# Layer 1's shift and scale columns: eight PE row sums and VectorE steps replaced by one VectorE dot product per column

## The chip, the cores and the metric

The program runs on one core of one Trainium2 chip. TensorE is called PE here, VectorE DVE, ScalarE ACT, GpSimd POOL, and SyncE, whose queue issues nearly all loads, SP. The metric is the device time of one execution in microseconds (us); less is better.

## What is computed

Two decoder layers on 256 tokens of width 1024, both with the same frame: a modulation from the vector `c`, an RMS norm, a mixer, a gated residual. The change is in the modulation of the first layer (`i = 0`) and in the input projection of its mixer:

```python
for i in range(DEPTH):                                  # DEPTH = 2, D = 1024, SEQ = 256
    shift, scale, gate = jnp.split(c @ ada_w[i] + ada_b[i], 3, axis=-1)   # c: (1, 1024), ada_w[i]: (1024, 3072)
    h = rmsnorm(x, norm_g[i]) * (1.0 + scale[:, None, :]) + shift[:, None, :]
    ...
        y = nsa_mixer(h, a_w_in[li], ...)               # layer 0: q, kv, gate_logits, z = split(h @ w_in)
    ...
        y = mlstm_mixer(h, b_w_in[li], ...)             # layer 1
    x = x + gate[:, None, :] * y
return rmsnorm(x, final_g)
```

`shift` and `scale` are two vectors of 1024 numbers, each a dot product of `c` with a column of `ada_w[0]`. The kernel needs them transposed: for each of eight blocks `kk` of 128 channels, a column `[128, 2]` with the channel on the partition.

## The kernel before

The order of every engine's instructions in layer 1 is the order in which the code is written (`manual_schedule`); in layer 2 a scheduler sets it. Weights come in float32 through one stream, issued by SP in the order of `self.queue`. A load lands in one of ten buffers named `raw`, or in a guest place that is free at the time (`homes`: tiles `Q`, `KH`, `KL`), and waits for that buffer's last reader. For the matmuls each weight is split into a high part `wh` (ACT, line 162, `make_hi`) and a low part `wl` (DVE, line 167, `make_lo`), and so is the activation: `hh[:, kk]` high, `hl[:, kk]` low. A product is then three matmuls: `wh*hh`, `wl*hh`, `wh*hl`.

`setup` starts the loads of `x`, of `pca` (which holds `c` as eight columns, the norm weights and the biases of the modulation) and fills PE with idle matmuls (`warm`) of 512 columns each.

`first_phase` makes the norm and the projection `proj(kk)` for the eight blocks `kk` of 128 input channels. A block has 42 matmuls of 256 tokens at line 452: 24 for the 1024 outputs of the `q` weight (eight with `wh`, eight with `wl`, eight with `hl`), and 18 for the 768 outputs of the `s` weight. All of them sum into seven PSUM banks over the eight blocks. Before a block can start, its `hh[:, kk]` must be there, and for that its two columns `cols`.

The columns are made in three ways:

- Block 0: the weights of shift and scale (`opening`, input channel on the partition) are multiplied by `crep` (each number of `c` repeated 32 times) on PE, sixteen narrow matmuls in `ada_rows` (line 224) that leave four partial rows in four groups of partitions; a DVE copy; and a matmul with `sel` (line 471) that sums the groups and turns the row into a column.
- Block 1: the same inside block 0's matmuls (after matmul 21 `ada_rows`, after matmul 26 the turn at line 534, then `hh[:, 1]` on DVE).
- Blocks 2 to 7: `rows` (lines 405, 407). The weights (`pairs`, two loads of 512 KB per block) hold, per input channel on the partition, 128 shifts and 128 scales for each of four groups of input channels. Two ACT steps and six DVE steps multiply the eight groups by their number of `c` and sum them into two tiles `adaA` `[128, 256]`; line 512 adds the two. `columns` sums over the partitions with two PE matmuls with `ones1` (line 413), and two ACT steps (lines 415, 416) add the bias and scale. In block `kk` this is done for block `kk + 1`, the PE part after matmul 28 (32 in block 1). `modulate` then makes `hh[:, kk + 1]` on ACT (line 420).

After the eighth block the keys and values follow (`kv_block`, lines 593 to 595 and 1636 to 1638, weights `keys`), then the attention and layer 2.

Of the kernel before, what the change touches and what calls it, by code (L numbers as in the profile page):

```python
# [11 lines left out]
AF = mybir.ActivationFunctionType  # L12
OP = mybir.AluOpType
# [10 lines left out]
class Kernel:  # L24
# [223 lines left out]
    def setup(self):  # L248
# [13 lines left out]
        self.warm(10)  # L262
# [58 lines left out]
    def layer1(self):  # L321
        nc, t, pc, p1 = self.nc, self.t, self.pc, self.p1
        ident = self.ident
        self.stream_init()
        place = [[] for _ in range(KC)]

        def ada(kk):
            if kk > 1:
                self.pairs_stream(kk)
            else:  # L330
                self.cols_stream(kk)
            if kk:
# [36 lines left out]
        self.small_loads()  # L369

        with self.tc.manual_schedule(engines={mybir.EngineType.PE, mybir.EngineType.Activation, mybir.EngineType.DVE, mybir.EngineType.Pool, mybir.EngineType.SP}):
            self.first_phase(place)
            self.nsa(self.acc)
            self.boundary()

    def first_phase(self, place):
# [6 lines left out]
        self.warm(8)  # L383
# [15 lines left out]
        def rows(A, n):  # L399

            raw = self.take_raw(1)[0]
            for j in range(4):
                w, c, acc = raw[:, j].rearrange("p b m -> p (b m)"), pca[:, 4 * n + j : 4 * n + j + 1], A[:, j % 2]
                if not n and j < 2:
                    nc.scalar.activation(acc, w, AF.Copy, scale=c)
                else:
                    nc.vector.scalar_tensor_tensor(acc, w, c, acc, op0=OP.mult, op1=OP.add)

        def columns(kk, A):

            bank = self.bank(7)
            for b in (1, 0):
                nc.tensor.matmul(bank[:, b : b + 1], A[:, 0, b * P : b * P + P], self.ones1, start=True, stop=True, skip_group_check=True)
# [28 lines left out]
        def proj(kk):  # L442
# [3 lines left out]
            for i, m in ((0, 0), (0, 1), (0, 2), (1, 0), (1, 2), (1, 1)) if 0 < kk < KC - 1 else ((0, 0), (0, 1), (0, 2), (1, 0), (1, 1), (1, 2)):  # L446
# [35 lines left out]
        nc.vector.tensor_copy(*copies[1])  # L482
# [5 lines left out]
        A1 = self.T(pc, [P, 512], tag="adaA", bufs=2)  # L488
        for kk in range(KC):

            if not kk:
                self.make_lo(*wide)
# [4 lines left out]
            ahead = 0 < kk < KC - 1  # L497
            if ahead:
                A = self.T(pc, [P, 512], tag="adaA", bufs=2).rearrange("p (h m) -> p h m", h=2)
            if kk > 1 and ahead:  # L500
                rows(A, 0)
# [4 lines left out]
            if kk == 1:  # L506
                rows(A, 0)
            if kk == 1:
                wide = self.make_hi(place[kk][1])
            if ahead:  # L510
                rows(A, 1)
                nc.vector.tensor_tensor(A[:, 0], A[:, 0], A[:, 1], op=OP.add)
            if kk == 1:
                self.make_lo(*wide)
            elif kk:
                self.make(place[kk][1])
# [7 lines left out]
            for n, _ in enumerate(proj(kk)):  # L524
                if (kk, n) == (7, 8):
                    parameters()
                if not kk and n == 21:
                    bank, raws = self.bank(7), self.take_raw(2)
                    self.ada_rows(bank, raws, SEQ)
                    nc.vector.tensor_copy(A1[:, 0:SEQ], bank[:, 0:SEQ])  # L530
                if not kk and n == 26:
                    cols, bank = self.T(pc, [P, 2], tag="cols", bufs=4), self.bank(7)
                    for b in (1, 0):
                        nc.tensor.matmul(bank[:, b : b + 1], A1[:, b * P : b * P + P], self.sel[:, 0:1], start=True, stop=True, skip_group_check=True)
                    for b in (1, 0):
                        column(bank, cols, b, 1)
                    nc.vector.tensor_scalar(self.hh[:, 1], xT[:, 1], cols[:, 1:2], cols[:, 0:1], op0=OP.mult, op1=OP.add)
                    self.make_lo(*parts)
                elif 0 < kk < KC - 1 and n == (32 if kk == 1 else 28):
                    cols = columns(kk + 1, A)  # L540
# [477 lines left out]
    def cols_stream(self, kk):  # L1018

        for b in range(2):  # L1020
            self.add(None, [P, KC, P], self.t["opening"][2 * kk + b])
# [5 lines left out]

    def pairs_stream(self, kk):

        for h in range(2):  # L1030
            self.add(None, [P, 4, 2, P], self.t["pairs"][2 * (kk - 2) + h])
# [646 lines left out]
def layout(inputs):  # L1678
# [17 lines left out]
    out["opening"] = flat([modulation[0][:, :, b, P * kk : P * kk + P] for kk in range(2) for b in range(2)])  # L1696
    out["pairs"] = flat([modulation[0][:, 4 * h : 4 * h + 4, :, P * kk : P * kk + P] for kk in range(2, KC) for h in range(2)])
# [22 lines left out]
```

## Time and profile before

| | |
|---|---|
| median of 3 runs | 443.38 us (442.69 to 443.74) |
| the profiled execution | 442.93 us, its span from the first to the last instruction 441.1 us |
| PE busy | 431.9 us, 98% of the span |
| DVE busy | 338.5 us, 77% |
| ACT busy | 279.0 us, 63% |
| blocks 0 to 7 of the projection | 12.92 to 58.87 us of the span |
| keys and values | 58.87 to about 78 us |

The profile shows one execution, in us from the start of its span. A group's row has the line, engine, operation, tiles and shapes, the count, the busy time, the mean ns of one, and the idle time of the engine just ahead with what ended it. A row of the timeline has start, duration, engine, line and count; the square bracket has the idle time ahead and its releaser. A table of windows has, for each stretch, its length and each engine's busy time with the number of instructions. PE durations overlap, since matmuls are pipelined; a price on PE is therefore taken from start to start. A float32 matmul shows as two rows (its count in the profile is twice that in the program), a matmul of the split parts as one.

### The profile page before, as it was taken

The numbers are of one execution on the slowest core, as the hardware profiler recorded it, in microseconds if no ns is written. First come the engines' busy times: TensorE is split into PE (matmuls) and PEld (weight loads), VectorE is DVE, ScalarE is ACT, GpSimd is POOL, SyncE is SP. The second block draws the span as 40 slices with busy tenths as digits, with TensorE's granted clock in tenths as the row PEclk, the third lists the DMA queues.
The fourth block names the chain that finished last, engine by engine and source line by source line (L and its number), as shares of the span: only waits on it lengthen the run. The fifth ranks groups of instructions, "written<-read, shape, count | busy, mean of one in ns | idle before, by whom it ended". The sixth has DMA issues, their size and how long they took to land.

```text
span 441.1 us, 8017 instructions
## 1 busy us (share of the span) xinstructions
PE 431.9 (98%) x2919; PEld 369.5 (84%) x2919; DVE 338.5 (77%) x771; ACT 279.0 (63%) x563; POOL 37.6 (9%) x92
## 2 busy tenths in 40 slices
PE   8999999999999999999999999999999999999993
PEld 3999999689578877788899799988888888888883
DVE  4899899788787677788995398789886977558553
ACT  4677693876887786459657775554665565455521
POOL 4000030224232020021000000000000000000000
PEclk9999999999999999999999999999999999999997
DMA  8999877782387777826864536638646766530002
GB/s 281 417 415 419 299 239 245 276 315 66 124 318 275 285 270 253 289 103 207 292 211 152 164 123 219 208 128 269 227 143 189 258 243 230 183 137 1 0 1 96
DMA packets 27031, 94.56 MB, mean 214 GB/s; under 512 B 3216, under 2 KB 3232, under 8 KB 26992
## 3 DMA queue, kind: packets, MB, share of 16 engines
q1 hardware_dynamic: 26352, 92.30, 59.3%
q0 software_dynamic: 352, 0.97, 0.8%
q10 hardware_dynamic: 288, 0.79, 0.7%
q8 instruction: 23, 0.38, 0.3%
q14 instruction: 16, 0.13, 0.1%
HBM read 93.00 MB, written 1.05 MB: 213 GB/s over the span
## 4 chain that ended last, share of the span: by engine, by line
PE 89%; DVE 4%; DMA 3%; ACT 1%; issue 1%; SPq 0%; DVEq 0%
PE bank L595 10%; PE bank L593 10%; PE bank L594 10%; PE bank L1638 6%; PE bank L1637 6%; PE bank L1636 6%; PE bank L914 5%; PE bank L1547 5%; PE bank L1077 5%; PE bank L1191 4%; PE bank L452 3%; PE bank L224 3%; PE bank L866 3%; PE bank L849 3%; DMA raw<-in_keys 2%; PE bank L1427 2%
## 5 line engine op out<-in xcount | busy, mean ns | idle before, releaser
L167 DVE TENSOR_TENSOR wl<-raw,wh 128x1024 fp32r<-128x1024 f32 (+4 forms) x127 | 137.3, 1099 | 40.2 <-ACT wh L162 39.3
L162 ACT ACTIVATE wh<-raw 128x1024 fp32r<-128x1024 f32 (+4 forms) x127 | 118.6, 956 | 64.1 <-PE bank L595 30.4
L593 PE MATMUL bank<-wh,one 128*128 128x512 f32 (+1 forms) x208 | 76.9, 370 | 0.0
L594 PE MATMUL bank<-wl,one 128*128 128x512 f32 (+1 forms) x208 | 76.4, 367 | 0.0
L595 PE MATMUL bank<-wh,one 128*128 128x512 f32 (+1 forms) x208 | 76.4, 368 | 0.0
L1636 PE MATMUL bank<-one,wh 128*128 128x256 f32 x208 | 59.7, 287 | 0.0
L1638 PE MATMUL bank<-one,wl 128*128 128x256 f32 x208 | 59.4, 285 | 0.1
L1637 PE MATMUL bank<-one,wh 128*128 128x256 f32 x208 | 59.1, 284 | 0.0
L593 PEld LDWEIGHTS bank<-wh,one 128*128 128x128 f32 x208 | 39.3, 189 | 6.2 <-DVE tz L565 0.3
L595 PEld LDWEIGHTS bank<-wh,one 128*128 128x128 f32 x208 | 39.2, 189 | 6.1
L594 PEld LDWEIGHTS bank<-wl,one 128*128 128x128 f32 x208 | 39.3, 189 | 5.9
L1638 PEld LDWEIGHTS bank<-one,wl 128*128 128x128 f32 x208 | 39.8, 191 | 0.5 <-DVE wl L167 0.3
L1637 PEld LDWEIGHTS bank<-one,wh 128*128 128x128 f32 x208 | 39.9, 192 | 0.1
L1636 PEld LDWEIGHTS bank<-one,wh 128*128 128x128 f32 x208 | 39.8, 192 | 0.1
L452 PE MATMUL bank<-one,wh 128*128 128x256 f32 x224 | 31.8, 287 | 0.1
L830 ACT ACTIVATE Pr<-Pr,mn 128x128 f32<-128x128 f32 (+1 forms) x64 | 28.2, 447 | 1.8 <-DVE mn L823 1.7
L452 PEld LDWEIGHTS bank<-one,wh 128*128 128x128 f32 x224 | 28.6, 192 | 0.5 <-ACT one L420 0.3
L844 POOL TENSOR_SCALAR Pr<-Pr,f 128x128 f32<-128x128 f32 (+1 forms) x24 | 18.8, 798 | 47.9 <-DVE f L838 34.9
L1408 DVE SCALAR_TENSOR_TENSOR conv<-bank,one,conv 128x255 f32<-128x255 f32 (+2 forms) x48 | 20.2, 473 | 2.1 <-ACT conv L1403 2.1
L823 DVE CUSTOM_DVE_ANT_0 Pr<-bank,one 128x128 f32<-128x128 f32 (+1 forms) x64 | 18.8, 352 | 3.3 <-PE bank L809 2.1
L677 ACT ACTIVATE PT<-bank 128x384 f32<-128x384 f32 x32 | 14.5, 486 | 8.3 <-PE bank L849 8.3
L914 PE MATMUL bank<-wh,Q 128*128 128x512 f32 x48 | 16.7, 406 | 0.0
(352 smaller groups left out, 803.9 us busy)
## 6 DMA issues: line engine op xcount, KB each, us to landing
raw<-in_wide SPq DMA_DIRECT2D x44, 512.0 KB, 4.4
raw<-in_units SPq DMA_DIRECT2D x18, 512.0 KB, 4.2
raw<-in_gates SPq DMA_DIRECT2D x16, 512.0 KB, 5.7
raw<-in_turn SPq DMA_DIRECT2D x16, 512.0 KB, 6.3
raw<-in_out_b SPq DMA_DIRECT2D x16, 512.0 KB, 3.5
raw<-in_start SPq DMA_DIRECT2D x8, 512.0 KB, 9.4
raw<-in_hidden SPq DMA_DIRECT2D x8, 512.0 KB, 4.3
raw<-in_path SPq DMA_DIRECT2D x8, 512.0 KB, 4.5
```

What stands on the lines that cost most here:

```text
L162: self.nc.scalar.activation(v(hi), src, AF.Copy)
L167: self.nc.vector.tensor_sub(v(lo), src, v(hi).bitcast(F32))
L452: nc.tensor.matmul(out, w[:, ch * P : ch * P + P], h[:, kk], start=(kk == 0 and m == 0 and ch % 2 == 0), stop=(kk == 7 and m == 2), skip_g ...
L593: nc.tensor.matmul(out, self.hh[:, kk, sl], wh, start=first, stop=False, skip_group_check=True)
L594: nc.tensor.matmul(out, self.hh[:, kk, sl], wl, start=False, stop=False, skip_group_check=True)
L595: nc.tensor.matmul(out, self.hl[:, kk, sl], wh, start=False, stop=last, skip_group_check=True)
L830: nc.scalar.activation(v, v, AF.Exp, bias=mn[:, a, br, j : j + 1], scale=-1.0, accum_out=sm[:, a, br, j : j + 1])
L914: nc.tensor.matmul(out, l[:, sl], w[:, c0:c1], start=(k == 0 and m == 0), stop=(k == 7 and m == 2), skip_group_check=True)
L1077: ins = nc.tensor.matmul(out, l[:, sl], w[:, c0:c1], start=(k == 0 and m == 0), stop=(k == N - 1 and m == 2), skip_group_check=True)
L1636: nc.tensor.matmul(out, wh, self.hh[:, kk], start=first, stop=False, skip_group_check=skip)
L1637: nc.tensor.matmul(out, wh, self.hl[:, kk], start=False, stop=False, skip_group_check=skip)
L1638: nc.tensor.matmul(out, wl, self.hh[:, kk], start=False, stop=last, skip_group_check=skip)
```

## The change

Block 0 keeps its way. For blocks 1 to 7 the weights of shift and scale are laid out transposed on the host (`columns`): the output channel on the partition, all 1024 input channels along the free dimension, one load of 512 KB for shift and one for scale. `c` is broadcast once to all partitions: eight PE matmuls of a repeated column of `pca` with the identity (line 381 of the new code), two DVE copies of 512 (line 382) into `cbc` `[128, 1024]`. Each column is then one DVE instruction over 1024 elements that multiplies the weights by `cbc`, scales, adds the bias and sums along the free dimension (line 405 of the new code; with the reading of the accumulator it is two entries). `rows`, the sum of the two tiles, the matmuls with `ones1`, the two ACT steps and block 1's own way are gone, and with them `pairs_stream`. In the program every block makes the columns of the next one right after its `hl[:, kk]`, and `modulate` for the next block stands after matmul 28 in block 0 too.

Moved with it: the number of idle matmuls at the start (10 and 8 become 7 and 4, then 1 and 2 become 2 and none); the scaling of the other 896 channels of `x` stands ahead of block 0's columns; the copies of the transposed `x` that DVE made go to ACT; the low part of block 0's `s` weight stands after the first columns; in block 0 the matmuls with `hl` stand ahead of those with `wl` for the `s` weight; and in the stream of loads the columns of block `kk + 1` stand after both weights of block `kk`.

```diff
@@ setup @@
-        self.warm(10)
+        self.warm(7)
@@ layer1: the order of the loads @@
         def ada(kk):
-            if kk > 1:
-                self.pairs_stream(kk)
-            else:
-                self.cols_stream(kk)
+            self.cols_stream(kk)
...
             weights(kk, "q")
-            if kk:
-                ada(kk + 1)
             weights(kk, "s")
-            if not kk:
-                ada(kk + 1)
+            ada(kk + 1)
@@ first_phase @@
         nc.vector.tensor_copy(self.crep, pca[:, 0:8].unsqueeze(2).to_broadcast([P, 8, 32]))
-        self.warm(8)
+        self.cbc = self.T(pc, [P, D], tag="gate")
+        for h in range(2):
+            b = self.bank(5 + 2 * h)
+            for k in range(4):
+                nc.tensor.matmul(b[:, k * P : k * P + P], pca[:, 4 * h + k : 4 * h + k + 1].to_broadcast([P, P]), ident, start=True, stop=True, skip_group_check=True)
+            nc.vector.tensor_copy(self.cbc[:, 512 * h : 512 * h + 512], b)
+        self.warm(4)
...
         scaled(slice(0, P))
+        scaled(slice(P, D))
...
-        def columns(kk, A):
-
-            bank = self.bank(7)
-            for b in (1, 0):
-                nc.tensor.matmul(bank[:, b : b + 1], A[:, 0, b * P : b * P + P], self.ones1, start=True, stop=True, skip_group_check=True)
+        def columns(kk):
+
             cols = self.T(pc, [P, 2], tag="cols", bufs=4)
-            nc.scalar.activation(cols[:, 1:2], bank[:, 1:2], AF.Identity, bias=pca[:, 24 + kk : 25 + kk], scale=pca[:, 8 + kk : 9 + kk])
-            nc.scalar.activation(cols[:, 0:1], bank[:, 0:1], AF.Identity, bias=pca[:, 16 + kk : 17 + kk])
+            for b, raw in enumerate(self.take_raw(2)):
+                scale = pca[:, 8 + kk : 9 + kk] if b else 1.0
+                nc.vector.tensor_tensor_reduce(raw, raw, self.cbc, scale, pca[:, 16 + 8 * b + kk : 17 + 8 * b + kk], OP.mult, OP.add, cols[:, b : b + 1])
             return cols
...
-            for i, m in (...) if 0 < kk < KC - 1 else (...):
+            for i, m in (...) if kk < KC - 1 else (...):
...
-        self.warm(1)
+        self.warm(2)
...
-        scaled(slice(P, D))
-        self.warm(2)
...
-        nc.vector.tensor_copy(*copies[1])
-        nc.vector.tensor_copy(*copies[3])
         self.guests_in = True
         wide = self.make_hi(place[0][1])
-        nc.scalar.activation(*copies[2], AF.Copy)
+        for n in (1, 3, 2):
+            nc.scalar.activation(*copies[n], AF.Copy)
...
         for kk in range(KC):
...
-            if kk > 1 and ahead:
-                rows(A, 0)
             if kk:
                 h32 = self.T(p1, [P, SEQ], tag="y32", bufs=2)
                 modulate(kk, h32, cols)
                 rest(kk, h32)
...
-            if ahead:
-                rows(A, 1)
-                nc.vector.tensor_tensor(A[:, 0], A[:, 0], A[:, 1], op=OP.add)
-            if kk == 1:
+            if kk < KC - 1:
+                following = columns(kk + 1)
+            if kk:
+                self.make(place[kk][1])
+            else:
                 self.make_lo(*wide)
-            elif kk:
-                self.make(place[kk][1])
...
-                if not kk and n == 21:
-                    bank, raws = self.bank(7), self.take_raw(2)
-                    self.ada_rows(bank, raws, SEQ)
-                    nc.vector.tensor_copy(A1[:, 0:SEQ], bank[:, 0:SEQ])
-                if not kk and n == 26:
...
-                elif 0 < kk < KC - 1 and n == (32 if kk == 1 else 28):
-                    cols = columns(kk + 1, A)
+                if kk < KC - 1 and n == 28:
+                    cols = following
                     modulate(kk + 1, self.hh[:, kk + 1], cols)
                     self.make_lo(*parts)
@@ layout, on the host @@
-    out["pairs"] = flat([modulation[0][:, 4 * h : 4 * h + 4, :, P * kk : P * kk + P] for kk in range(2, KC) for h in range(2)])
+    out["columns"] = a["ada_w"][0][:, : 2 * D].reshape(D, 2, KC, P).transpose(2, 1, 3, 0)[1:]
```

How this moves instructions, at three places. In the names of tiles the number at the end is a serial number.

DVE in block 1, from the low part of `h` (`one_6_69` is `hl`) to the low part of block 2's `q` weight. Before:

```order
L429 TENSOR_TENSOR one_6_69<-y_103_373,one_4_68 128x256
L407 SCALAR_TENSOR_TENSOR adaA_372<-Q_194,one_8_70,adaA_372 128x256 x2
L407 SCALAR_TENSOR_TENSOR adaA_372<-Q_196,one_8_70,adaA_372 128x256 x4
L512 TENSOR_TENSOR adaA_372<-adaA_372 128x256
L167 TENSOR_TENSOR wl_389<-raw_198,wh_388 128x768
L167 TENSOR_TENSOR wl_400<-raw_200,wh_399 128x1024
```

The same place after the change (`gate_148` is `cbc`):

```order
L418 TENSOR_TENSOR one_6_69<-y_106_364,one_4_68 128x256
L405 ISA Q_204,cols_367<-Q_204,gate_148,one_8_70 128x1024
L405 ISA cols_367 128x1
L405 ISA Q_206,cols_367<-Q_206,gate_148,one_8_70 128x1024
L405 ISA cols_367 128x1
L167 TENSOR_TENSOR wl_371<-raw_202,wh_370 128x768
L167 TENSOR_TENSOR wl_375<-raw_208,wh_374 128x1024
```

Seven steps of 256 elements (and two on ACT ahead of them) have become two of 1024, each with its accumulator read; the two `wl` stand behind them as before.

PE in the second half of block 1, where the `s` weight (`wh_388`, `wl_389`) is multiplied. Before:

```order
L452 MATMUL bank_282<-one_4_68,wh_388 128x256 x2
L452 MATMUL bank_280<-one_6_69,wh_388 128x256 x2
L452 MATMUL bank_281<-one_6_69,wh_388 128x256
L413 MATMUL bank_441<-one_14_89,adaA_372 128x1 x2
L452 MATMUL bank_281<-one_6_69,wh_388 128x256
L452 MATMUL bank_282<-one_6_69,wh_388 128x256 x2
L452 MATMUL bank_280<-one_4_68,wl_389 128x256 x2
```

The same place after the change:

```order
L441 MATMUL bank_288<-one_4_68,wh_370 128x256 x2
L441 MATMUL bank_286<-one_6_69,wh_370 128x256 x2
L441 MATMUL bank_287<-one_6_69,wh_370 128x256 x2
L441 MATMUL bank_288<-one_6_69,wh_370 128x256 x2
L441 MATMUL bank_286<-one_4_68,wl_371 128x256 x2
```

The two matmuls with `ones1` that stood between the products are gone; nothing on PE stands between the 42 matmuls of a block any more.

SP, the stream of loads from the columns of block 1 to the `q` weight of block 2. Before:

```order
L86 DMA Q_188<-in_opening 128x1024
L86 DMA Q_190<-in_opening 128x1024
L86 DMA raw_192<-in_start 128x1024
L86 DMA Q_194<-in_pairs 128x1024
L86 DMA Q_196<-in_pairs 128x1024
L86 DMA raw_198<-in_start 128x768
L86 DMA raw_200<-in_start 128x1024
```

The same place after the change:

```order
L86 DMA Q_196<-in_columns 128x1024
L86 DMA Q_198<-in_columns 128x1024
L86 DMA raw_200<-in_start 128x1024
L86 DMA raw_202<-in_start 128x768
L86 DMA Q_204<-in_columns 128x1024
L86 DMA Q_206<-in_columns 128x1024
L86 DMA raw_208<-in_start 128x1024
```

The `s` weight of block 1 (128x768) has moved ahead of the two loads for block 2's columns; the bytes up to block 2's `q` weight are the same.

More of the change, by code (lines that the diff above doesn't have):

```diff
@@ L396, in first_phase @@
         scaled(slice(0, P))
+        scaled(slice(P, D))
         nc.vector.scalar_tensor_tensor(pca[:, 24:32], pca[:, 24:32], 1.0, pca[:, 8:16], op0=OP.add, op1=OP.mult)
[L399 to L407, printed above, removed]
-        def columns(kk, A):
-            bank = self.bank(7)
-            for b in (1, 0):
-                nc.tensor.matmul(bank[:, b : b + 1], A[:, 0, b * P : b * P + P], self.ones1, start=True, stop=True, skip_group_check=True)
+        def columns(kk):
             cols = self.T(pc, [P, 2], tag="cols", bufs=4)
-            nc.scalar.activation(cols[:, 1:2], bank[:, 1:2], AF.Identity, bias=pca[:, 24 + kk : 25 + kk], scale=pca[:, 8 + kk : 9 + kk])
-            nc.scalar.activation(cols[:, 0:1], bank[:, 0:1], AF.Identity, bias=pca[:, 16 + kk : 17 + kk])
+            for b, raw in enumerate(self.take_raw(2)):
+                scale = pca[:, 8 + kk : 9 + kk] if b else 1.0
+                nc.vector.tensor_tensor_reduce(raw, raw, self.cbc, scale, pca[:, 16 + 8 * b + kk : 17 + 8 * b + kk], OP.mult, OP.add, cols[:, b : b + 1])
             return cols
@@ L445, in proj @@
             parts = [self.take(hold=n > 0) for n in range(2)]
-            for i, m in ((0, 0), (0, 1), (0, 2), (1, 0), (1, 2), (1, 1)) if 0 < kk < KC - 1 else ((0, 0), (0, 1), (0, 2), (1, 0), (1, 1), (1, 2)):
+            for i, m in ((0, 0), (0, 1), (0, 2), (1, 0), (1, 2), (1, 1)) if kk < KC - 1 else ((0, 0), (0, 1), (0, 2), (1, 0), (1, 1), (1, 2)):
                 n, c0 = cols[i]
@@ L496, in first_phase @@
                     nc.gpsimd.dma_start(dst, src)
-            ahead = 0 < kk < KC - 1
-            if ahead:
-                A = self.T(pc, [P, 512], tag="adaA", bufs=2).rearrange("p (h m) -> p h m", h=2)
-            if kk > 1 and ahead:
-                rows(A, 0)
             if kk:
@@ L505, in first_phase @@
                 rest(kk, h32)
-            if kk == 1:
[L507 to L510, printed above, removed]
-                rows(A, 1)
-                nc.vector.tensor_tensor(A[:, 0], A[:, 0], A[:, 1], op=OP.add)
-            if kk == 1:
+            if kk < KC - 1:
[3 more added lines that the diff above has]
+            else:
                 self.make_lo(*wide)
-            elif kk:
-                self.make(place[kk][1])
             if 1 < kk < 5:
@@ L526, in first_phase @@
                     parameters()
-                if not kk and n == 21:
-                    bank, raws = self.bank(7), self.take_raw(2)
-                    self.ada_rows(bank, raws, SEQ)
-                    nc.vector.tensor_copy(A1[:, 0:SEQ], bank[:, 0:SEQ])
-                if not kk and n == 26:
[L532 to L538, printed above, removed]
-                elif 0 < kk < KC - 1 and n == (32 if kk == 1 else 28):
-                    cols = columns(kk + 1, A)
+                if kk < KC - 1 and n == 28:
+                    cols = following
                     modulate(kk + 1, self.hh[:, kk + 1], cols)
@@ L1020, in cols_stream @@
         for b in range(2):
-            self.add(None, [P, KC, P], self.t["opening"][2 * kk + b])
+            if kk:
+                self.add(None, [P, D], self.t["columns"][kk - 1, b])
+            else:
+                self.add(None, [P, KC, P], self.t["opening"][b])
     def turn_stream(self, s):
@@ L1026, in turn_stream @@
             self.add(None, [P, 4, 256], self.t["turn"][4 * s + k])
-    def pairs_stream(self, kk):
-        for h in range(2):
-            self.add(None, [P, 4, 2, P], self.t["pairs"][2 * (kk - 2) + h])
     def gate_stream(self, l, n):
@@ L1695, in layout @@
     out["gate_b"] = a["b_gate_b"][0].T
-    out["opening"] = flat([modulation[0][:, :, b, P * kk : P * kk + P] for kk in range(2) for b in range(2)])
-    out["pairs"] = flat([modulation[0][:, 4 * h : 4 * h + 4, :, P * kk : P * kk + P] for kk in range(2, KC) for h in range(2)])
+    out["opening"] = flat([modulation[0][:, :, b, :P] for b in range(2)])
+    out["columns"] = a["ada_w"][0][:, : 2 * D].reshape(D, 2, KC, P).transpose(2, 1, 3, 0)[1:]
     out["turn"] = flat([modulation[1][:, 4 * h : 4 * h + 4, b, 256 * s : 256 * s + 256] for s in range(4) for b in range(2) for h in range(2)])
```

3 lines of the change are left out of this document (removed).

## The prediction

> **What bounds the kernel now.** I read the page first (busy shares, slices), then a table of windows by block, then the timeline inside a block, then the loads.
>
> ```profile
> PE 431.9 (98%) x2919; PEld 369.5 (84%) x2919; DVE 338.5 (77%) x771; ACT 279.0 (63%) x563; POOL 37.6 (9%) x92
> PE   8999999999999999999999999999999999999993
> GB/s 281 417 415 419 299 239 245 276 315 66 124 318 275 285 270 253 289 103 207 292 211 152 164 123 219 208 128 269 227 143 189 258 243 230 183 137 1 0 1 96
> ```
>
> PE is busy from end to end, so what leaves PE's queue leaves the time, unless something else ends last there. The loads run at 415 to 419 GB/s in slices 2 to 4 (11 to 44 us), a level reached nowhere later. By blocks:
>
> ```profile
> 12.92:19.69 6.77, 6.77 (x81) 6.44 (x80) 5.21 (x12) 4.15 (x8) 0.00 (x0) 1.00 1.03 415
> 19.69:25.38 5.69, 5.63 (x48) 5.43 (x46) 5.39 (x12) 3.15 (x7) 0.00 (x0) 1.00 1.03 421
> 25.38:31.29 5.91, 5.84 (x47) 5.64 (x48) 5.32 (x10) 4.67 (x11) 0.73 (x1) 1.00 1.03 414
> 36.92:42.55 5.63, 5.63 (x49) 5.55 (x47) 5.32 (x10) 4.39 (x11) 0.00 (x0) 1.00 1.03 417
> 53.83:58.87 5.04, 5.04 (x45) 5.04 (x43) 4.29 (x6) 4.48 (x9) 1.84 (x3) 1.00 0.79 278
> 58.87:78.00 19.13, 18.98 (x148) 18.22 (x148) 18.30 (x27) 12.16 (x19) 3.05 (x7) 1.00 0.79 236
> ```
>
> The columns after the length are PE, PEld, DVE, ACT, POOL, granted clock, DMA share, GB/s. The rows are blocks 0, 1, 2, 4, 7, and the keys and values. Block 7, which makes no columns, takes 5.04 us: 42 matmuls at 0.12. Block 4 takes 5.63, with PE never idle. The difference is this:
>
> ```profile
> 15.72 1.08 PE L224 MATMUL bank<-Q,one 128*32 128x128 f32 x32
> 16.73 0.86 PE L452 MATMUL bank<-one,wh 128*128 128x256 f32 x5
> 17.43 0.53 PE L534 MATMUL bank<-one,adaA 128*128 128x1 f32 x4
> 17.82 0.37 PE L452 MATMUL bank<-one,wh 128*128 128x256 f32 x1
> 40.44 0.61 PE L413 MATMUL bank<-one,adaA 128*128 128x1 f32 x4
> 40.91 1.08 PE L452 MATMUL bank<-one,wh 128*128 128x256 f32 x7
> 25.38 1.01 PEld L452 LDWEIGHTS bank<-one,wh 128*128 128x128 f32 x8 [0.27 <-ACT one L420]
> 29.18 0.52 PEld L413 LDWEIGHTS bank<-one,adaA 128*128 128x128 f32 x4 [0.27 <-DVE adaA L512]
> ```
>
> From start to start, line 413 holds PE 40.91 - 40.44 = 0.47 us; block 1's columns hold it 1.01 (line 224) and 0.39 (line 534) within block 0. Block 2 waits 0.27 for its `hh`, and again 0.27 for `adaA`.
>
> **The change, part by part.** (1) PE loses line 413 six times (2.8 us), lines 224 and 534 in block 0 (1.4), and the two waits (0.5). What could be late next is DVE, ACT or a load.
>
> (2) DVE. The prices:
>
> ```profile
> L167 DVE TENSOR_TENSOR wl<-raw,wh 128x768 fp32r<-128x768 f32 x8 | 7.5, 951 | 0.0
> L167 DVE TENSOR_TENSOR wl<-raw,wh 128x1024 fp32r<-128x1024 f32 x6 | 7.3, 1219 | 0.5 <-ACT wh L162 0.5
> L407 DVE SCALAR_TENSOR_TENSOR adaA<-Q,one,adaA 128x256 f32<-128x256 f32 x18 | 7.6, 480 | 0.5 <-ACT adaA L405 0.5
> L512 DVE TENSOR_TENSOR adaA<-adaA 128x256 f32<-128x256 f32 x6 | 2.6, 426 | 0.2
> L1594 DVE CUSTOM_DVE_ANT_0 conv<-one 128x256 f32<-128x256 f32 x1 | 0.4, 424 | 0.0
> 82.99 0.28 DVE L823 CUSTOM_DVE_ANT_0 Pr<-bank,one 128x128 f32<-128x128 f32 x1
> 83.20 0.42 DVE L823 CUSTOM_DVE_ANT_0 Pr<-bank,one 128x256 f32<-128x256 f32 x1
> 83.55 0.08 DVE L823 DVE_READ_ACCUMULATOR2_ANT mn<- 128x1 f32 x1
> 83.55 0.42 DVE L823 CUSTOM_DVE_ANT_0 Pr<-bank,one 128x256 f32<-128x256 f32 x1
> ```
>
> The new instruction is that of line 1594, which takes 424 ns for 256 elements of two float32 tiles, as a plain sum of two tiles (line 512: 426). Its accumulator read hides under the next one (83.55 twice). From start to start 128 elements take 0.21 and 256 take 0.35, so 1024 take 0.35 + 6 x 0.135 = 1.16 us; a scalar read from a tile costs some 0.05 more each (line 407 against 512), which makes 2.47 for the two columns. The low bound is 2.3 (no price for the scalars), the high bound half speed, 4.6; I take 2.47, since both rows of this very operation say so. Taking 0.07 off each duration for overlap, a block of DVE is 0.35 (`hl`) + 2.47 + 0.88 + 1.15 (`wl`) = 4.85 us, against 5.32 busy now and under PE's 5.06. ACT falls from 4.39 by lines 405, 415 and 416; it is no limit.
>
> The Trainium skill, "Vector Engine (DVE) Microarchitecture Reference" (its list of pitfalls), states that a scalar-tensor-tensor shape with two sources in SBUF that are not bf16 runs at half throughput, because both read ports are taken and none is left for the accumulator. By that rule the pair would take the 4.6 us of the high bound. Line 1594, with two float32 sources in SBUF and an accumulator, shows no halving, though both its sources are one tile; so the trace speaks against the rule here.
>
> (3) Loads. Landings show where ACT waits for them:
>
> ```profile
> 15.61 1.15 ACT L162 ACTIVATE wh<-raw 128x512 fp32r<-128x512 f32 x2 [1.00 <-DMA raw<-in_start]
> 20.44 0.85 ACT L162 ACTIVATE wh<-raw 128x768 fp32r<-128x768 f32 x1 [0.66 <-DMA raw<-in_start]
> 21.70 1.06 ACT L162 ACTIVATE wh<-raw 128x1024 fp32r<-128x1024 f32 x1 [0.40 <-DMA raw<-in_start]
> ```
>
> These are block 1's `q` weight, its `s` weight, and block 2's `q` weight. A block's loads are 4 x 512 KB less 128 KB = 1.97 MB, at 417 GB/s 4.71 us: shorter than 5.06, by little. SP's new order brings the `s` weight two loads earlier (2.5 us) and each pair of columns one 384 KB load later (0.94 us); block 2's `q` weight keeps its bytes ahead of it and lands at 21.7 as now. That is the new limit at the front: ACT splits it (21.7 to 22.7), then makes `hh` for block 2 behind it in its queue (0.6), so block 2 cannot start before 23.3. Its columns (last load about 20.4, two DVE steps, done 21.6) are ready by then. Later `q` weights land every 4.71 us (26.4, 31.1, 35.8 ...) and lead PE by 0.35 us more in each block; the chance of a wait falls with every block.
>
> (4) The start.
>
> ```profile
> 4.39 0.29 DVE L382 COPY one<-one 128x256 f32<-128x256 f32 x1 [1.44 <-DMA one<-in_first]
> 6.07 0.15 PEld L246 LDWEIGHTS <-y 128*128 128x128 bf16 x1 [0.28 <-issue]
> 6.50 0.97 PEld L246 LDWEIGHTS <-y 128*128 128x128 bf16 x5 [0.28 <-issue]
> 8.49 0.65 PE L224 MATMUL bank<-raw,one 128*32 128x128 f32 x16 [0.53 <-DVE rq_y L209]
> 12.92 1.20 PE L452 MATMUL bank<-one,wh 128*128 128x256 f32 x8
> 123.46 0.86 PE bank L900 x2
> L482 DVE COPY xT<-bank 128x512 f32<-128x512 f32 x1 | 0.7, 685 | 0.0
> ```
>
> The idle matmuls of 512 columns start every 0.43 us until 6.5 and every 0.21 after it: PE doubles its speed there, though the granted clock reads 1.00 throughout. `c` lands at 4.39. The eight new products are float32, 128 columns: line 900 shows 0.86 for 512 columns at full speed, so 0.215 each, 1.7 us in all, or 3.4 at the slow pace. Half and half, they end at about 7.2, the second DVE copy (0.69, line 482) at 8.0; the norm's steps behind it on DVE (from 7.94) are not held up. The four `warm` matmuls write the bank that this copy reads, so PE waits 0.8 us for it, and behind them stand `ada_rows` and the transposes: `ada_rows` starts at 8.9 instead of 8.49. Since one `warm` fewer follows, and DVE has scaled `x` already, block 0 starts at 12.75 instead of 12.92 by this count; I bound it by -0.5 and +1.6 (all products slow). Up to 0.5 us late costs nothing, because block 2 waits for its load anyway.
>
> (5) Block 0. DVE does `hh`, `wl`, `hl` (until 14.1), then the two columns (loads at 13.1 and 14.3; until 16.5), then `wl` of the `s` weight until 17.3. The products with that `wl` are now the last six, due at 12.75 + 36 x 0.12 = 17.07: a wait of some 0.25. Block 0 ends at 18.05 (now 19.69), block 1 at 23.1, block 2 starts at 23.3 (now 25.38).
>
> The sum against the trace: start -0.17, block 0 -1.47, block 1 with its wait -0.44, block 2 -0.85, blocks 3 to 6 -0.57 each, block 7 zero: **-5.2 us**; block 7 ends at 53.65 instead of 58.87. Behind it the same instructions stand in the same order on all engines. The keys are loaded by then (16.8 MB are ahead of them by the sizes in the code, landed at about 46 at 417 GB/s, and the keys at 1 us each), and in the stretch of the keys DVE and PE go side by side (18.30 and 18.98 of 19.13), so both shift. Nothing after it runs at 415 GB/s. I carry the whole 5.2 on. The profiled time is 442.93, 0.45 below the median of 443.38; 5.2 less gives 437.7 by the one and 438.2 by the other. I say 438.0.
>
> **The rivals.** (a) The loads take part of it back: a skew of the landings by 1 to 2 us, as between 15.61 and 20.44 (4.8 us for 3.5 us' worth of bytes), falls on a weight and holds blocks 2 to 4, or the keys' stretch keeps some. Against it: the lead grows per block. That leaves 3 to 4 us: 439 to 440.5. (b) The speed of PE doubles later. The switch came 5.3 us after the first matmul; if the pause for the copy starts the count anew at 8.0, it comes at 13.3, everything ahead of block 0 is slow, and block 0 starts 3.5 us late; of this block 2's load hides 0.5, so 2.2 of the gain is left: 441. For it: the new pause of 0.8; against it: PE's idle 0.53 ahead of line 224 had no such effect. The Trainium skill, "TensorE: Matmul & The Clock Gate" (Part 1), gives a window of about 3.4 us that runs freely, after which a busy PE is let go to full clock and an idle one is held back; by that a pause of 0.8 us does nothing, and the switch may come earlier or later by some 3 us; the trace agrees as far as the 0.53 goes. (c) Slower: the new instruction runs at half speed. DVE needs 0.35 + 4.6 + 0.88 + 1.15 = 7.0 us in a block and becomes the bound from 5.06 on: six blocks at 7.0 instead of 5.69 on average (19.69 to 53.83) add 7.9, block 0 ends 0.5 later: 451. It decides when the pair takes more than 3.2 us, where DVE's block equals today's 5.63. (d) PE's time goes into waits further back and nothing is left: 443. The unbroken 9s of PE speak against it.
>
> **How the numbers follow.** Forecast 0.70, (a) 0.14, (b) 0.06, (c) 0.04, (d) 0.04, something slower that I don't see 0.02. The likeliest alone: 437.0 to 439.0. The range of 8 in 10 takes in most of (a): 436.6 to 440.6. Faster by over 0.2% (about the least that a measurement of this kernel can tell): forecast, (a), most of (b): 0.88; within it 0.05; slower 0.07.
>
> **What the profile after would show.** Blocks of 5.06 us from block 2 on with PE at 42 matmuls and no idle; the new DVE rows at about 1.25 us; `hh` of block 2 after its `q` weight at 23.3; DVE at 4.8 of a block; the keys' stretch 19.1 us as now, from about 53.7. Wrong it is if the DVE rows exceed 1.6 us, if ACT waits for `in_start` after block 3, or if block 0 starts after 13.5.

## The result, and the profile after

The changed kernel takes 437.54 us (median of 4 runs, 437.13 to 437.76), the kernel before, run beside it, 443.56 (442.69 to 444.24). The ratio is 0.9864, with a 95% interval of 0.9845 to 0.9884. The profiled execution took 437.76 us with a span of 436.0, so its span is 5.1 us shorter than that of before.

The same three rows of the page, for the changed kernel:

```profile
PE 426.7 (98%) x2867; PEld 366.5 (84%) x2867; DVE 337.4 (77%) x753; ACT 272.3 (62%) x542; POOL 37.4 (9%) x92
PE   7999999999999999999999999999999999999993
GB/s 285 417 417 418 400 253 197 372 200 50 254 303 221 245 332 279 258 96 240 271 188 168 150 137 210 195 141 280 197 148 197 281 238 218 183 135 0 2 0 97
```

PE lost 52 records and 5.2 us of busy time and, from the second slice on, is as unbroken as it was. Slice 5 now has 400 GB/s where it had 299: the loads did not fall behind the shorter blocks. The table of windows by block (length, then PE, PEld, DVE, ACT, POOL, clock, DMA share, GB/s), for blocks 0, 1, 2, 4 and 7 and for the keys and values:

```profile
13.27:18.82 5.55, 5.37 (x46) 5.17 (x45) 5.55 (x10) 5.05 (x10) 0.00 (x0) 1.00 1.02 414
18.82:23.85 5.03, 5.03 (x44) 5.03 (x43) 5.03 (x8) 2.56 (x5) 0.00 (x0) 1.00 1.02 418
23.85:28.89 5.04, 5.04 (x44) 5.04 (x43) 5.04 (x10) 3.39 (x6) 0.73 (x1) 1.00 1.03 420
33.93:38.97 5.04, 5.04 (x44) 5.04 (x43) 5.04 (x9) 2.97 (x5) 0.00 (x0) 1.00 1.03 419
49.05:54.09 5.04, 5.04 (x44) 5.04 (x43) 2.70 (x5) 2.59 (x6) 1.82 (x3) 1.00 1.03 402
54.09:73.20 19.11, 18.98 (x148) 18.27 (x148) 18.34 (x26) 12.25 (x19) 3.06 (x6) 1.00 0.78 254
```

From block 1 on every block is as long as block 7: 42 matmuls and nothing else. The first block starts 0.35 us later than before and is 1.22 shorter; block 1 gives 0.66, block 2 0.87, blocks 3 to 6 0.59 each (5.63 became 5.04). The keys start at 54.09 instead of 58.87, so 4.8 us earlier, and their stretch keeps its 19.1 us. Nothing behind them gives any of it back; the span is 5.1 us shorter, and for the 0.3 beyond 4.8 no run here has a reason.

DVE reads busy for the whole of blocks 0 to 5 and for 5.00 of 5.04 us in block 6. Its timeline in block 4 tells what that is worth:

```profile
33.85 1.28 DVE L405 CUSTOM_DVE_ANT_0 Q<-Q,gate,one 128x1024 f32<-128x1024 f32 x1
35.06 0.09 DVE L405 DVE_READ_ACCUMULATOR2_ANT cols<- 128x1 f32 x1
35.06 1.35 DVE L405 CUSTOM_DVE_ANT_0 Q<-Q,gate,one 128x1024 f32<-128x1024 f32 x1
36.32 2.10 DVE L167 TENSOR_TENSOR wl<-raw,wh 128x768 fp32r<-128x768 f32 x2
38.33 0.42 DVE L418 TENSOR_TENSOR one<-y,one 128x256 fp32r<-128x256 f32 x1
38.66 1.28 DVE L405 CUSTOM_DVE_ANT_0 Q<-Q,gate,one 128x1024 f32<-128x1024 f32 x1
```

From start to start the two columns take 36.32 - 33.85 = 2.47 us, and a whole block of DVE 38.66 - 33.85 = 4.81, against 5.04 of PE. DVE does not rest because it works ahead by 0.23 us in each block, not because it holds PE up.

The loads, as ACT sees them land, and the use of the first of them in block 2:

```profile
21.57 1.06 ACT L162 ACTIVATE wh<-raw 128x1024 fp32r<-128x1024 f32 x1 [2.47 <-DMA raw<-in_start]
22.53 0.59 ACT L409 ACTIVATE one<-xT,cols 128x256 fp32r<-128x256 f32 x1
23.85 1.12 PE L441 MATMUL bank<-one,wh 128*128 128x256 f32 x8
26.30 1.06 ACT L162 ACTIVATE wh<-raw 128x1024 fp32r<-128x1024 f32 x1 [1.65 <-DMA raw<-in_start]
```

Block 2's `q` weight lands at 21.57, its `hh` is made at 22.53 to 23.1, and PE, still in block 1, takes it at 23.85: PE waits for no load. The next `q` weight lands 4.73 us later.

### The profile page after: what moved, and what is told of

The parts are those of the page before. It is cut to its first block, busy times and chain, and to the rows that moved or that the text cites. A ratio compares the mean times of both kernels' runs of the same rounds, so it can differ in the third digit from the quotient of the medians.

```text
span 436.0 us, 7878 instructions
## 1 busy us (share of the span) xinstructions
PE 426.7 (98%) x2867; PEld 366.5 (84%) x2867; DVE 337.4 (77%) x753; ACT 272.3 (62%) x542; POOL 37.4 (9%) x92
## 4 chain that ended last, share of the span: by engine, by line
PE 93%; DVE 2%; DMA 1%; issue 1%; ACT 1%; SPq 0%; DVEq 0%
PE bank L556 10%; PE bank L554 10%; PE bank L555 10%; PE bank L441 8%; PE bank L1597 6%; PE bank L1596 6%; PE bank L1595 6%; PE bank L875 5%; PE bank L1506 5%; PE bank L1036 5%; PE bank L1150 4%; PE bank L224 3%; PE bank L827 3%; PE bank L810 3%; PE bank L1386 2%; PE bank L767 2%
## 5 line engine op out<-in xcount | busy, mean ns | idle before, releaser
L1595 PE MATMUL bank<-one,wh 128*128 128x256 f32 x208 | 59.6, 286 | 0.0
L1596 PE MATMUL bank<-one,wh 128*128 128x256 f32 x208 | 59.0, 284 | 0.0
L441 PE MATMUL bank<-one,wh 128*128 128x256 f32 x224 | 29.7, 283 | 0.0
```

The source lines that it names most:

```text
L441: nc.tensor.matmul(out, w[:, ch * P : ch * P + P], h[:, kk], start=(kk == 0 and m == 0 and ch % 2 == 0), stop=(kk == 7 and m == 2), skip_g ...
L1595: nc.tensor.matmul(out, wh, self.hh[:, kk], start=first, stop=False, skip_group_check=skip)
L1596: nc.tensor.matmul(out, wh, self.hl[:, kk], start=False, stop=False, skip_group_check=skip)
```

## The experiments

The theory: the gain is PE time that left the queue (line 413 and block 1's own columns), the columns cost DVE 2.47 us a block and fit under PE, and the start and the order of the loads matter little. The rivals: the moves at the start carry the gain, the loads hold part of it back, or DVE is already the bound. Where a run is set against the changed kernel, their medians are compared, though the two ran at different times; measured by the kernel before that ran beside each, these differences change by less than 0.2 us.

### The moves at the start alone, on the kernel before

```diff
         scaled(slice(0, P))
+        scaled(slice(P, D))
...
-        self.warm(1)
+        self.warm(2)
...
-        scaled(slice(P, D))
-        self.warm(2)
...
-        nc.vector.tensor_copy(*copies[1])
-        nc.vector.tensor_copy(*copies[3])
...
-        nc.scalar.activation(*copies[2], AF.Copy)
+        for n in (1, 3, 2):
+            nc.scalar.activation(*copies[n], AF.Copy)
```

> The kernel before with the reordered start alone: all of x scaled ahead of block 0's columns, one idle matmul fewer, the copies of the transposed x on ACT; the columns as before. Theory (the gain is PE work taken out of the blocks): the start is worth nothing, 443.6 within 0.5 us. Rival (the reordered start is a good part of the gain): 442 or less.

443.32 us against 443.72, ratio 0.9986 (0.9977 to 0.9996). The start is not where the gain comes from: it is worth 0.4 us between the medians, 0.2 to 1.0 by the interval. Its timeline has block 0 later than in the profile of before, though:

```profile
8.01 1.06 ACT L390 ACTIVATE KL<-one 128x1024 f32<-128x1024 f32 x1 [2.51 <-DMA one<-in_x]
13.67 1.20 PE L453 MATMUL bank<-one,wh 128*128 128x256 f32 x8
```

```profile
6.76 1.06 ACT L390 ACTIVATE KL<-one 128x1024 f32<-128x1024 f32 x1 [1.33 <-DMA one<-in_x]
```

The second half of `x` landed at 8.01 here and at 6.76 in the profile of before (second fence). Block 0 follows the landing by 5.66 us, where before it took 12.92 - 6.76 = 6.16. So the moves save 0.5 in the profile, where a late landing hid it. The next runs bear on that.

### PE's part put back

Two one-column float32 matmuls, as line 413 had, after matmul 28 of blocks 1 to 6; DVE's part stays new.

```diff
                 if kk < KC - 1 and n == 28:
+                    if kk:
+                        bank = self.bank(7)
+                        for b in (1, 0):
+                            nc.tensor.matmul(bank[:, b : b + 1], self.cbc[:, b * P : b * P + P], self.ones1, start=True, stop=True, skip_group_check=True)
                     cols = following
```

> The changed kernel with the two matmuls of one column put back on PE after matmul 28 of blocks 1 to 6 (they sum the broadcast c; nobody reads the result). Theory (PE is the bound of a block): each costs the 0.47 us that line 413 took, so 6 x 0.47 = 2.8 us more than the changed kernel, about 440.4, and blocks of 5.5 us. Rival (the loads or DVE end last in a block, at 4.7 to 4.8): 0.2 to 0.3 us a block are hidden, at most 1.5 us more, 439.

440.20 us, ratio 0.9919 (0.9904 to 0.9934): 2.7 us more than the changed kernel. PE's timeline in one block:

```profile
37.75 1.24 PE L441 MATMUL bank<-one,wh 128*128 128x256 f32 x9
38.83 0.50 PE L504 MATMUL bank<-one,gate 128*128 128x1 f32 x4
39.19 1.08 PE L441 MATMUL bank<-one,wh 128*128 128x256 f32 x7
40.82 1.12 PE L441 MATMUL bank<-one,wh 128*128 128x256 f32 x8
```

The two matmuls (four rows, line 504) hold PE for 0.36 from start to start, and a block grew from 5.04 to 5.47: the other 0.07 lies in the matmuls around them. Six times 0.43 is 2.6. This is the largest single term of the gain.

It is not all of it: a block of the kernel before took 5.63, 0.16 more than this one. The rows point to a wait. The first two are from the kernel before (DVE's sum of the two tiles, then PE's loading of it as weights), the third from this run:

```profile
39.96 0.42 DVE L512 TENSOR_TENSOR adaA<-adaA 128x256 f32<-128x256 f32 x1
40.44 0.52 PEld L413 LDWEIGHTS bank<-one,adaA 128*128 128x128 f32 x4
38.71 0.53 PEld L504 LDWEIGHTS bank<-one,gate 128*128 128x128 f32 x4
```

Here the weights begin to load 0.12 us ahead of their first matmul (38.71 and 38.83). In the kernel before they began together with it, at 40.44, just behind the end of DVE's sum (39.96 + 0.42 = 40.38), and it is so in blocks 2 to 6. Part of what the prediction counted as PE's work there was thus probably PE waiting for DVE; no run separates the two.

### A quarter and three quarters of a step more on DVE

A sum of two tiles of 256 elements behind the columns in blocks 0 to 6, once, and in another kernel three times.

```diff
                 following = columns(kk + 1)
+                spare = self.T(p1, [P, 256], tag="spare")
+                nc.vector.tensor_tensor(spare, self.cbc[:, 0:256], self.cbc[:, 0:256], op=OP.add)
```

> The changed kernel with one more DVE step of 256 elements (0.35 us from start to start) behind the two columns of each of blocks 1 to 7. Theory (DVE needs 4.81 of PE's 5.04 us in a block and runs 0.4 us ahead at block 1, more later): 0.35 later in block 0, then 5.16 against 5.04 with the lead eating most of it: 0.3 to 0.8 us more, about 438.1. Rival (DVE has room): no change, 437.5.

> The same with three DVE steps of 256 elements (1.04 us) in each of blocks 1 to 7, as if a pair of columns took 3.5 us in place of 2.47. Theory: DVE becomes the bound with 5.85 us a block; 1.04 later in block 0 and 6 x 0.81 less a lead of 0.4: 5.5 us more than the changed kernel, 443.0, that is the gain gone and blocks of 5.85 us. It tests the point from which the change would not have paid (a pair of 3.2 us by the prediction). Rival (PE's 42 matmuls still set the block): 437.5 to 439.

One sum: 438.85 us, ratio 0.9888 (0.9873 to 0.9903), 1.3 more than the changed kernel. DVE in its block 4:

```profile
34.70 1.28 DVE L405 CUSTOM_DVE_ANT_0 Q<-Q,gate,one 128x1024 f32<-128x1024 f32 x1
37.16 0.42 DVE L487 TENSOR_TENSOR spare<-gate 128x256 f32<-128x256 f32 x1
39.84 1.28 DVE L405 CUSTOM_DVE_ANT_0 Q<-Q,gate,one 128x1024 f32<-128x1024 f32 x1
```

DVE's block is 39.84 - 34.70 = 5.14 us and PE's 5.15 (its blocks start at 29.03, 34.18, 39.33, 44.48): with 0.33 more DVE is the bound. From block 0's start to block 7's end 41.9 us pass instead of 40.82. I had expected 0.3 to 0.8, since I took DVE to have a lead to use up; it has hardly one, since block 0 already waits for it (below).

Three sums: 445.18 us, ratio 1.0029 (1.002 to 1.0039), slower than the kernel before. DVE and PE in its block 3:

```profile
34.06 1.33 DVE L488 TENSOR_TENSOR spare<-gate 128x256 f32<-128x256 f32 x3
35.31 2.08 DVE L167 TENSOR_TENSOR wl<-raw,wh 128x768 fp32r<-128x768 f32 x2
36.32 0.98 PE L441 MATMUL bank<-one,wl 128*128 128x256 f32 x6 [0.77 <-DVE wl L167]
```

The sums take 1.25, so DVE's block is 4.81 + 1.25 = 6.06, and PE, at 6.07 a block, waits 0.77 for `wl` of the `s` weight. The expectation of 443.0 had put 1.04 on the three sums. Between the two kernels the time grows 6.33 us for 0.92 of DVE; on a straight line between them it reaches the 443.5 of the kernel before with about 1.0 us more than now, a pair of columns of some 3.5 us.

### The old order of loads

```diff
             weights(kk, "q")
+            if kk:
+                ada(kk + 1)
             weights(kk, "s")
-            ada(kk + 1)
+            if not kk:
+                ada(kk + 1)
```

> The changed kernel with the loads in the old order: from block 1 on, the columns of the next block between the q and the s weight. Theory (the order of the loads is worth nothing: the s weight comes 2.5 us later, at 25.1 for block 2, and its low part is made behind the columns at 26.7 anyway): 437.5 within 0.5 us. Rival (the new order is a part of the gain): 1 us or more slower, with PE waiting for the s weight in blocks 1 to 3.

437.54 us, ratio 0.9867 (0.9854 to 0.988): the order of the loads is worth nothing that these runs can tell. Its profile has `x` at 6.77, as before had it, and so shows the start of the changed kernel without the late landing:

```profile
6.77 1.06 ACT L393 ACTIVATE KL<-one 128x1024 f32<-128x1024 f32 x1 [1.29 <-DMA one<-in_x]
12.37 1.20 PE L444 MATMUL bank<-one,wh 128*128 128x256 f32 x8
17.92 1.12 PE L444 MATMUL bank<-one,wh 128*128 128x256 f32 x8
23.01 1.12 PE L444 MATMUL bank<-one,wh 128*128 128x256 f32 x8
```

Block 0 starts at 12.37, 0.55 ahead of before, and the profiled time is 436.94.

### The second half of x from another queue

```diff
-        nc.sync.dma_start(self.x[:, 1], xr[:, 1])
+        nc.scalar.dma_start(self.x[:, 1], xr[:, 1])
```

> The changed kernel with the load of the second half of x issued from ACT's queue as its first instruction instead of third on SP. In six profiles this half landed between 6.35 and 8.0 us, and block 0 started between 12.0 and 13.4 with it. Theory (the start hangs on this landing, and block 2 then on its q weight, which lands at 21.6): it lands before 6.4, block 0 starts at 12.0 or earlier, block 2 not before 23.0; 0.4 to 0.8 us less than the changed kernel, 436.9. Rival (both halves share the same bandwidth, so that the sum of the start stays): 437.5.

439.46 us (438.05 to 439.8), ratio 0.9908 (0.9892 to 0.9924): 1.9 more than the changed kernel, so the idea fell. Both halves of `x` were there at about 5.5, but `c` came with them, at 5.9 instead of 4.4, and PE stood still for it:

```profile
5.96 2.02 PE L381 MATMUL bank<-one,one 128*128 128x128 f32 x16 [1.61 <-DMA one<-in_first]
```

The norm then queued behind the copies of `cbc` on DVE, and block 0 started at 13.53. The profiled execution, at 438.05, is the lowest of the five; what the others lost besides it doesn't show. That PE's speed doubled later in them, after the pause of 1.61, would fit the runs on the clock below, but is only argued.

### PE's pause before the norm

The four idle matmuls behind the broadcast products write another bank than the one that DVE copies.

```diff
-        self.warm(4)
+        self.warm(4, 4)
```

> The changed kernel with the four idle matmuls behind the broadcast of c writing into another bank, so that PE does not wait 0.78 us for the second DVE copy. Theory (the first products wait for the norm of x, not for PE): no change, 437.5 within 0.4. Rival (the pause holds the start, or the clock of PE): 0.4 to 0.8 us less.

437.36 us (437.06 to 440.24), ratio 0.9886 (0.9856 to 0.9917): no change that these runs can tell. In the changed kernel PE stands idle for 0.78 us there (first row; the second is the landing of `x` in the same profile, the third block 0):

```profile
8.11 1.02 PE L246 MATMUL bank<-y 128*128 128x512 bf16 x4 [0.78 <-DVE gate L382]
7.67 1.06 ACT L390 ACTIVATE KL<-one 128x1024 f32<-128x1024 f32 x1 [2.21 <-DMA one<-in_x]
13.27 1.20 PE L441 MATMUL bank<-one,wh 128*128 128x256 f32 x8
```

Without the pause block 0 started at 12.37 with `x` at 6.78, so 5.59 behind it, and with it 5.60 behind: the landing sets the start, the pause does not.

### Less work for PE

This kernel leaves out part of the sum: the six products with the low part of the `s` weight in each of blocks 1 to 6. That is 36 matmuls of 0.12 in all, so 4.3 us of PE, and it leaves 36 of the 42 in each of these blocks.

```diff
+                if 0 < kk < KC - 1 and (i, m) == (1, 1):
+                    continue
                 n, c0 = cols[i]
```

> The changed kernel without the six products of the s weight's low part in blocks 1 to 6 (left out of the sum): 36 matmuls, 4.32 us of PE in a block. It shows what comes next behind PE. Theory (DVE needs 4.81 us, a block's loads 4.71): blocks of 4.8 us, not 4.32, ended by DVE; 6 x 0.23 = 1.4 us less than the changed kernel, 436.1. Rival (PE is alone at the end of a block): 6 x 0.72 = 4.3 us less, 433.2.

435.49 us, ratio 0.9824 (0.981 to 0.9837): of 4.3 us only 2.05 arrive. PE's first products with `wl` in blocks 4, 5 and 6 come 4.81 us apart, and PE waits for DVE in front of them:

```profile
33.14 1.22 PE L443 MATMUL bank<-one,wl 128*128 128x256 f32 x8
37.95 1.22 PE L443 MATMUL bank<-one,wl 128*128 128x256 f32 x8 [0.15 <-DVE wl L167]
42.76 1.22 PE L443 MATMUL bank<-one,wl 128*128 128x256 f32 x8 [0.16 <-DVE wl L167]
```

The 36 matmuls of a block alone would be 4.31. DVE's 4.81 is the next bound, as its timeline said. The 1.4 us expected took 4.81 for every block; the first one still took 4.31 (its products with `wl` start at 19.27, the next block's at 23.58), which is most of the rest.

### The clock at the start, three kernels and the changed one again

The idle matmuls ahead of the broadcast are left out (first), left out with no pause behind the products (second), or three instead of seven with no pause (third).

```diff
@@ first @@
-        self.warm(7)
@@ second @@
-        self.warm(7)
...
-        self.warm(4)
+        self.warm(4, 4)
@@ third @@
-        self.warm(7)
+        self.warm(3)
...
-        self.warm(4)
+        self.warm(4, 4)
```

> The seven idle matmuls ahead of the broadcast of c are left out, so PE's first matmul comes at about 4.5 us instead of 1.2. Theory: the doubling of PE's speed is counted from the first busy PE work, 5.3 us as in all profiles so far, so it comes at about 9.8: the eight products all run at the slow pace and end at 8.0 instead of 7.2, the second DVE copy ends at 8.9, the transposes run partly slow, block 0 starts about 1.0 to 1.5 us later than with them (13.2 to 15 by the landing of x), blocks stay at 5.04, and the time is 438.3 to 439.3. Rival: the doubling comes at 6.3 us from the start of the span whatever PE does: block 0 starts as with the idle matmuls and the time is 437.0 to 437.8. Second rival, PE that was idle is held back for several us more: switch after 12, everything ahead of block 0 slow, 440 or more.

> The changed kernel again, unedited, as yardstick beside the other and for the spread of the landing of x. Theory: x's second half lands anywhere from 6.3 to 8.0 us, block 0 starts 0.3 to 1.1 us after the 12.0 of the earliest (12.0 to 13.7), blocks 1 to 7 at 5.04 each, and the time is 437.0 to 438.0. Rival, the late landing of 7.67 belongs to the changed kernel: it lands at 7.5 to 8.0 again and block 0 starts at 13.2 or later.

> Without the seven idle matmuls, as in the run before, but the four idle matmuls behind the products write a bank that no DVE copy reads, so PE has no pause of 0.78 us while it is slow. In the run with the pause PE's speed doubled at about 12.2 us, 7.7 us after its first matmul at 4.5, where with the seven idle matmuls it doubles 5.2 after the first (6.4). Theory: an idle stretch in the slow time starts the count anew, and 5.2 us of unbroken work are wanted: the doubling comes at 9.7, block 0 starts at 13.0 to 14.3 by the landing of x, and the time is 438.0 to 439.0. Rival, the count hangs on something other than the pause: the doubling stays at about 12.2, block 0 starts at 14.5 to 15.4, 439.0 to 440.3.

> Three idle matmuls ahead of the broadcast of c instead of seven, so that PE stands idle from about 2.6 to 4.5 us, and then no pause. Theory (an idle stretch starts the count anew): the doubling comes at 9.7 as without any idle matmuls, block 0 at 13.0 to 14.3, 438.0 to 439.0. Rival (idle time of 1.9 us is only left out of the count, or the count runs from the first matmul): the doubling comes at 6.4 to 8.3, block 0 starts as with all seven, and the time is 437.0 to 437.9.

The first took 439.79 us (438.26 to 440.26; ratio 0.9911, 0.9885 to 0.9936), the changed kernel beside it 437.55 (0.9868, 0.9853 to 0.9883), the second 437.73 (0.9874, 0.9851 to 0.9896), the third 438.01 (0.9878, 0.986 to 0.9895). PE's timeline, in this order the first, the second and the third kernel:

```profile
9.03 1.87 PE L246 MATMUL bank<-y 128*128 128x512 bf16 x4 [0.78 <-DVE gate L381]
10.82 1.08 PE L224 MATMUL bank<-raw,one 128*32 128x128 f32 x16
11.84 0.89 PE L246 MATMUL bank<-y 128*128 128x512 bf16 x2
```

```profile
7.78 1.91 PE L246 MATMUL bank<-y 128*128 128x512 bf16 x4
9.63 0.64 PE L224 MATMUL bank<-raw,one 128*32 128x128 f32 x16
```

```profile
4.43 3.75 PE L381 MATMUL bank<-one,one 128*128 128x128 f32 x16 [1.78 <-DMA one<-in_first]
7.97 1.91 PE L246 MATMUL bank<-y 128*128 128x512 bf16 x4
9.82 0.71 PE L224 MATMUL bank<-raw,one 128*32 128x128 f32 x16
```

Line 224 takes 0.64 at full speed and 1.08 at the slow pace. In the second kernel PE is fast by 9.63, in the third from about 9.9, though there PE had begun at 1.19: it looks as if the idle 1.78 us started the wait anew. Each of these is one profile. In the first kernel, with the pause of 0.78 in its slow time, PE is slow until about 12.3, and block 0 starts at 15.36, 7.7 behind the landing of `x` (7.62) instead of 5.6. So a pause in the slow time costs about 2 us by the medians, though the intervals of the first and the second kernel just overlap and one run of the first took 438.26; the same pause behind the doubling costs nothing that shows.

The expectation's "5.3 us as in all profiles" was wrong, and the 439.79 of the first kernel lay above the 438.3 to 439.3 expected. With 16 rows of line 381 at 0.11 or 0.21 each, the length of that group tells when PE doubled: 2.81 us in the changed kernel (about 6.3), 2.51 when it ran again (5.6), 2.02 with three sums (4.7), 3.07 without the pause (6.8). The doubling moves by 2 us from run to run with the same work ahead; the 9.9 of the third kernel lies 3.1 beyond the latest of these.

The changed kernel, run again, had `x` at 7.16 and block 0 at 12.76, 5.60 later, so the landing at 7.67 does not belong to the change.

## Why the prediction was right, point by point

**PE's time** (the first part). Right in size: blocks 3 to 6 gave 0.59 each for 0.57, and putting the matmuls back cost 2.7 for 2.8. Of the 0.59 the matmuls themselves are 0.43; the other 0.16 looks like a wait for `adaA`, which the prediction saw in block 2 alone.

**The new DVE step.** Right to the hundredth: 2.47 us a pair, an accumulator read of 0.09 that hides, 4.81 for 4.85 a block. The Trainium skill's rule in "Vector Engine (DVE) Microarchitecture Reference" (Points that are easy to get wrong), half speed for a scalar-tensor-tensor step with two SBUF sources that are not bf16, does not show in this instruction, now with two different float32 tiles: 1024 elements take 1.21 and 1.26 from start to start, and at half speed they would have taken some 2.3 (an estimate, twice the 1.16 of the prediction). Whether this instruction is of the shape that the rule names, no trace here shows. Line 407 of the kernel before, which the profile calls SCALAR_TENSOR_TENSOR, took 0.42 for 256 elements (four of them from 27.00 to 28.70) where line 512's plain sum took 0.35, so it was not halved either. Where slower begins was put too early: 3.2 us a pair, by comparing DVE's block with today's 5.63 alone; the runs say about 3.5, for which there is a part of the reason in the profiles: the six blocks took 5.69 on average (19.69 to 53.83), and the start keeps its gain of 0.5.

**The loads.** The landings were right (21.57 for 21.7, then one every 4.7), the conclusion was not: block 2 was held by PE and not by its `q` weight, whose `hh` is done at 23.1 while PE comes at 23.85. With `x` landing early PE came at 23.01 in one run and 23.22 in another, near 23.3, and still no load stood in the way of `hh`; in the second DVE waited 0.28 for a column weight and block 1 took 5.30, which is rival (a) in small. I also named a sign badly. The view of the waits (us in total, times, longest) has

```profile
ACT wh L162 <- DMA raw<-in_start: 11.5, 8, 2.5
```

so ACT goes on waiting for loads after block 3, and it means nothing, since in block 2 it was 0.7 us ahead of PE and PE waited for no load.

**The start.** The mis-sized term: -0.17 was forecast, and the profile has +0.35. The time of the second half of `x` was taken as fixed at 6.76; it landed at 7.67, and between 6.35 and 8.01 in the profiles of kernels that load it from SP's queue. From the landing to block 0 it is 5.60 us now and was 6.16, so the moves are worth about -0.55, and the landing added 0.9 in the profiled run. This fits that the two profiled times differ by 5.2 and the medians by 6.0: the profile of before, at 442.93, lies below its median, and that of after is the slowest of its runs. With `x` at 6.77 (the old order of loads) the profiled time was 436.94, 6.0 below before.

**Block 0.** 5.55 us for the 5.30 forecast. The wait for `wl` of the `s` weight is there:

```profile
16.99 2.16 DVE L167 TENSOR_TENSOR wl<-raw,wh 128x768 fp32r<-128x768 f32 x3
18.00 0.98 PE L441 MATMUL bank<-one,wl 128*128 128x256 f32 x6 [0.18 <-DVE wl L167]
18.82 1.12 PE L441 MATMUL bank<-one,wh 128*128 128x256 f32 x8
```

The bracket says 0.18, but from start to start the twenty matmuls ahead take 2.73 for 2.40, so it costs 0.33; the first sixteen and the last six are 0.08 and 0.10 slower than 0.12 each. In block 1 the last six start 0.16 before the row of the twenty ends (20.73 + 2.56 = 23.29, and 23.13); a wait takes that overlap too, and the bracket does not count it.

**The sum.** Start +0.35, block 0 -1.22, block 1 -0.66, block 2 -0.87, blocks 3 to 6 -2.37: -4.77 for -5.2 at the keys, all carried to the end. The start and block 0 were put 0.77 too low, blocks 1 to 6 gave 0.33 more than forecast, so the errors cancel in part. The time of 438.0 was within 0.5 of the median, and some of that is luck: by the medians the gain is 6.0 for the 5.2 of the sum, and the start without the late landing, 0.4 better than forecast, is half of the difference.

**The rivals.** Slower by half speed of DVE, and nothing left over, are out by the rows above. (b), PE doubling later through the pause, did not happen, since PE had doubled before the pause; but its mechanism is real, as the first of the three kernels on the clock shows, at 2.2 us where 3.0 had been put on it. The Trainium skill, "TensorE: Matmul & The Clock Gate" (Part 1), has a free-running window of about 3.4 us whose place varies; the doubling 3.5 to 5.6 us after PE's first matmul in a run without a gap agrees with that. The prediction read from it that a pause of 0.8 us does nothing; that held behind the doubling and not ahead of it, where the doubling came at about 12.3 instead of 9.6. The runs don't show the window itself.

## What to carry to other kernels

Price a new instruction from the same operation in the trace, by the distance from start to start at two sizes, and add the fixed and the per-element part: that was exact here over a factor of four in size. When the bound engine is freed, ask for the next one by its start-to-start period over a block and not by its busy share: DVE read full at 5.04 and had 0.23 us to spare, and 0.33 more made it the bound. Before comparing two starts, look when the first load landed in each profile, and compare from there.

## What the hardware showed

The second half of `x`, the second big load of the kernel, landed between 6.35 and 8.01 us in the profiles of kernels that load it from SP's queue, whatever else was changed, and block 0 of the changed kernel followed it in most by 5.60. PE's doubling moved between about 4.7 and 6.8 us with the same instructions ahead of it, while the granted clock read 1.00 in them all the time. And three sums of 256 elements in a row took 1.25 us where one alone takes 0.33 or 0.34: they write one tile three times, but why each then costs 0.42 was not tried.
